# Normed tokens and gated values set off by several distances modulo 512 bytes from the weights they are multiplied with

## The chip, the cores and the metric

The kernel runs on one core of a Trainium2 chip. The metric is the device time of one execution in microseconds (us); the figure for a kernel is the median of several executions. The core has five engines that work side by side: TensorE (PE, with its weight loads shown apart as PEld), VectorE (DVE), ScalarE (ACT), GpSimd (POOL) and SyncE (SP), which here issues most of the DMA transfers. Data lies in SBUF, 128 partitions wide; TensorE takes both of its operands from there and writes to PSUM.

## The reference, cut to what matters

Two layers over 1024 latent and 256 context tokens, 1024 features wide, everything in fp32. What is multiplied is this:

```python
u = modulate(rms_norm(h, norm1_g), shift1, scale1)
p = u @ w_in                      # 1024 -> 2336 columns, cut into three mixers
y = ...                           # attention, long convolution, linear attention, a norm per head
h = h + gate1 * (y @ w_out)
u = modulate(rms_norm(h, norm2_g), shift2, scale2)
h = h + gate2 * ((silu(u @ ffn_w1) * (u @ ffn_w3)) @ ffn_w2)    # 1024 -> 2816 -> 1024
```

After the second layer a last norm gives the output for the latent tokens.

## The kernel before

**Products.** Features stand on partitions, in 8 chunks of 128. Every large product is made in three matmuls: each operand is split into a high and a low part in the format float32r (4 bytes an element), and `mm3` adds high by high, high by low and low by high. So a block of output, 128 features by up to 512 tokens, takes 8 chunks times 3, 24 matmuls, each with its own load of 128 by 128 weights (the stationary operand, 512 bytes a partition), while the tokens stream past (the moving operand, 2048 bytes a partition for 512 tokens). Tokens come in three blocks: 0 and 1 of 512 latent tokens, 2 of the 256 context tokens. The last layer has no context tokens in its second half.

**Tiles on the left side of SBUF.** Pools are opened and closed like a stack, and each begins where the one before it ends:

- `wts` (`open_w`): `hl`, two slots of 8 KB for streamed weights, high and low, and `raw`, 4 KB.
- `u0` (`open_u0`): the normed tokens of block 0, 32 KB.
- `u`: those of blocks 1 and 2, 32 KB and 16 KB.
- `w4`, in the second half of a layer alone (`phase34`): a third slot `hl` for `ffn_w1` and `ffn_w3`, two of `w2` for `ffn_w2`, and raw tiles.
- `g`, after it: the gated values silu(u w1) (u w3), high and low, two tiles.
- `w1`, in the first half of a layer (`phase1`): `tm`, weights of 288 columns that are the moving operand, with 128 tokens of `u` as the stationary one.

All these tiles are multiples of 512 bytes long, and so are their chunks, but for those of `tm`: 288 columns of 4 bytes are 1152 bytes, twice 512 and 128 more. So `hl`, `w2`, `u` and `g` begin at one and the same place modulo 512 bytes, and `tm` moves on by 128 from chunk to chunk.

**Stages.** For each layer `phase1` makes the input projection, `phase2` the three mixers, `phase34` the output projection (tiles `y`), the second norm and SwiGLU. In SwiGLU two hidden chunks are made (`hidden`: 24 matmuls of `u` by `hl` for each of w1 and w3 and each block), and their share of the output is added to the residual `h` (8 groups of 6 matmuls of `g` by `w2` a block). Every third weight tile of w1 and w3 goes to the slot in `w4`:

```python
for i, src in enumerate((A["ffn_w1"], A["ffn_w3"])):
    j = 2 * m + i
    ws.append(self.load_w(src[l][:, c], wp=wp if j % 3 == 2 else None, raws=wp if i else None))
```

Weights come by a DMA on SP's queue to `raw`; ScalarE makes the high part (L421), GpSimd the low part (L187), TensorE multiplies (L175). The order of the instructions on each engine is set by a scheduler in the framework, which simulates a timeline when the program is built. In the first layer VectorE also makes modulation vectors under SwiGLU (`ada_dve`, L329), which it sums over partitions by fp32 matmuls against ones (tiles `acc`, `ones`).

Of the kernel before, what the change touches and what calls it, by code (L numbers as in the profile page):

```python
# [17 lines left out]
P = 128  # L18
# [12 lines left out]
# columns of the combined input projection  # L31
C_Q, C_K, C_V, C_HY, C_GQ, C_GK, C_GV, C_GR, C_GF = 0, 512, 640, 768, 1536, 1664, 1792, 2048, 2304

# rows of the packed per-layer vectors
# [3 lines left out]
# ---------------------------------------------------------------- constants that depend on shapes alone  # L38
# [13 lines left out]
def _pk(m):  # L52
    """[T, K] -> [2, 128, T/128 * K]: exact parts, rows on partitions."""
    t, k = m.shape
    return np.stack([x.reshape(t // P, P, k).transpose(1, 0, 2).reshape(P, -1) for x in _hilo(m)])


def _consts():
    f = np.float64
    c = {}  # L60
# [25 lines left out]
    # rotations from the half-sample offset to offset 0, frequencies on partitions  # L86
# [37 lines left out]
class Builder:  # L124
# [20 lines left out]

    def ps(self, role=None):
        """a bank of PSUM: of a role, or of the current roles in turn."""
        role = self.role if role is None else role
        if role is None:
            role = self.cyc[self.nps % len(self.cyc)]  # L150
            self.nps += 1
        banks = self.banks[role]
        self.turn[role] = (self.turn[role] + 1) % len(banks)
        return self.psum.tile([P, 512], F32, name=self.nm("ps"), tag=f"ps{banks[self.turn[role]]}", bufs=1)

    def roles(self, *banks):
        """the banks of PSUM that each role takes in turn."""
        self.banks, self.turn = banks, [-1] * len(banks)

    def act_table(self, name):  # L160
        """one activation table set from here on: ScalarE's later instructions stay behind its load."""
# [11 lines left out]
    # -------------------------------------------------------------- small helpers  # L173
# [3 lines left out]
    def mm3(self, out, w, x, start, stop):  # L177
        """w, x: pairs (hi, lo); out += whi xhi + whi xlo + wlo xhi."""
# [10 lines left out]
    def rsqrt(self, pool, v, n, tag, eps=None, bufs=2):  # L189
        """-2 / sqrt(v + eps) for v [128, n] in PSUM: exp(-ln/2) and a Newton step."""  # L190
# [13 lines left out]
    # -------------------------------------------------------------- setup  # L204
# [42 lines left out]
    def vectors(self, vp, silb, ahead):  # L247
        """the conditioning vectors, biases and gains, features on partitions; other loads go ahead in between."""
        nc, A = self.nc, self.A
        for srcs in ((("c", None, 8), ("c_ctx", None, 8)),  # L250
# [22 lines left out]
            elif "filt_b1" in at:  # L273
                nc.vector.tensor_copy(self.fvec, ps[:, 0:3])
                # the norm gains scaled by -1/2: rsqrt() returns -2 / sqrt
# [6 lines left out]
    # -------------------------------------------------------------- adaLN vectors  # L282
# [10 lines left out]
    def ada_pe(self, l, part, wp, silb, ahead=()):  # L293
        """mod vectors: the conditioning vectors (16 columns each) stationary, weights moving; the rows of weights in
        turn on three column tiles."""
# [20 lines left out]
    def ada_dve(self, l, part, half, wp):  # L316
        """mod vectors of half a part: weighted rows summed on the vector engine; returns what sums the partitions."""
# [27 lines left out]
    # -------------------------------------------------------------- modulated norm: u (hi, lo) per block of tokens  # L345
    def norm_scale(self, l, which):
        """[128, 8, 2] gains: -1/2 g (1 + scale)."""
# [8 lines left out]
    def square(self, h, k, n, tp, acc):  # L356
        """adds the squares of chunk k of h [128, 8, n]; returns the sum so far, and whole, 1 / rms: tokens on partitions."""
# [23 lines left out]
    def spread(self, r, n, tp):  # L381
        """r [128, n / 128] -> -2 r of each token on all partitions, in PSUM."""
# [7 lines left out]
    def norm_u(self, h, u, scale, shift, r, tp, pool=(), tags=("s", "acc")):  # L390
        """u [128, 2, 8, n] F32R from h [128, 8, n]; r: -2 / rms; pool: the chunks whose low parts GpSimd makes."""
# [14 lines left out]
    # -------------------------------------------------------------- weights  # L406
    def load_w(self, src, n=P, wp=None, raws=None, lo_eng=None):
        """src [1024, n] -> (hi, lo) tile [128, 2, 8, n]."""
# [15 lines left out]
    # -------------------------------------------------------------- tokens in: feature-major residual  # L424
    def load_h(self, hp, xp):
        """features on partitions; yields after each block, with its -2 / rms on all partitions (PSUM)."""
# [35 lines left out]
    # -------------------------------------------------------------- hyena filters  # L462
    def sin_arg(self, pool, ps, b, fr, n):
        """sin(fr * (ps + b)) [128, n], the argument brought to [-pi, pi]."""
# [13 lines left out]
    def filter_mlp(self, fp, up):  # L478
        """hidden features of both layers' filters (a layer on 64 partitions), latent and context lengths, to DRAM."""
# [28 lines left out]
    def filter_body(self, l, kinds, fp):  # L508
        """spectra of one layer's filters to DRAM, latent ('l') and context ('c') lengths."""
# [5 lines left out]
        # X = [h_hi; h_lo], W1 = [w_hi; w_hi], W2 = w_lo  # L515
# [9 lines left out]
        def times(job):  # L525
            """the filter of a job in time, taken apart into folded levels."""
# [36 lines left out]
        def spectra(job, levels):  # L563
# [3 lines left out]
            for group in self.groups(levels):  # L567
                for pair, ps in self.transform(group, dft, fp):
                    for i, (L, k) in enumerate(pair):
# [20 lines left out]
                        else:  # L590
                            # cosine twice, or the two of the cyclic level; then the sine of either
# [26 lines left out]
    def start(self, hp, sp, up, tp, u):  # L618
        """tokens in, the first modulation vectors, the hidden features of the filters, the first norm."""
# [38 lines left out]
    # -------------------------------------------------------------- input projection  # L658
    def phase1(self, l):
        """norm 1, the input projection and what follows it token by token."""  # L660
# [3 lines left out]
        with ExitStack() as es:  # L664
            u = []
            if l == 0:
                self.open_w()
                self.open_u0()
            if l == 0:
                up = es.enter_context(self.pool("u", reuse_waits="tile"))  # L670
                hp = self.hpool.__enter__()
# [20 lines left out]
            # feature-major columns  # L692
# [11 lines left out]
            # hyena: short convolution  # L704
# [21 lines left out]
            # gated linear attention: gates (silu as x sigmoid(x)), queries, keys  # L726
# [47 lines left out]
    def open_w(self):  # L774
        """room of the streamed weights."""
# [8 lines left out]
    def open_u0(self):  # L784
        """room of the first block of the normed tokens."""
        self.u0p = self.pool("u0", 1, reuse_waits="tile")
        self.up0 = self.u0p.__enter__()

    def norm1(self, l, b, r, up):
        """norm 1 of a block of layer l > 0."""  # L790
# [4 lines left out]
    def load_tm(self, srcs, wp=None):  # L795
        """column groups side by side: [128, 2, 8, n]."""
# [15 lines left out]
    def tm(self, u, hl, n, tci):  # L812
        """tokens of chunk tci on partitions: [128, n] in PSUM."""
# [9 lines left out]
    def log_sigmoid(self, e, out, ps, m=None, b=None):  # L823
        """out = min(x, 0) - ln(1 + exp(-|x|)), x = ps + b; e, m: room."""
# [10 lines left out]
    def gla_prep(self, l, last, gv, tp, u):  # L835
# [27 lines left out]
        # decays: cumulative log gates of each chunk of 128 tokens, centred on its middle  # L863
# [4 lines left out]
        for d in range(2):  # L868
# [15 lines left out]
            # from the centre of a chunk to that of the next one  # L884
# [16 lines left out]
    def qkv(self, l, last, W, tp, u):  # L901
# [14 lines left out]
        def heads(ps, nh, which, tci, out, scale):  # L916
            """RMS norm, gain and rotation of nh heads: out [128, nh, 64]."""
# [7 lines left out]
            # scale / sqrt(ss / 64 + eps)  # L925
# [16 lines left out]
        def feature_major(xs, dst, c0):  # L942
            """token-major [128, 128] tiles of consecutive chunks from c0 on to dst [128, tokens] in DRAM."""
# [32 lines left out]
    # -------------------------------------------------------------- heads' norm and the mixed output  # L976
    def headnorm(self, tp, o, chunk, b0, n, l, v=None, gate=None, q=None):
        """o [128, n] (two heads of 64): RMS norm per head, gain, optional gate; to y_d. v: the mean squares if known."""
# [15 lines left out]
    # -------------------------------------------------------------- attention  # L994
    def attn_kv(self, ap, kvh):
        """operands of one kv head: K1 = [k_hi; k_lo], K2 = [k_hi; 1]."""
# [14 lines left out]
    def attn_q(self, ap, h, ops, b):  # L1011
        """operands of a block of queries: Q1 = [q_hi; q_hi], Q2 = [q_lo; -max]."""
# [27 lines left out]
    def attn_o(self, ap, ops, b, Q):  # L1040
        """softmax and values of a block of queries, two heads at once: the unnormalized outputs, one bank, and the
        sums of the weights over each partition's keys."""
# [28 lines left out]
    def attention(self, l, last, ap, np_):  # L1071
# [15 lines left out]
        for i, (kvh, pr, b) in enumerate(jobs):  # L1087
# [4 lines left out]
            # eps times the squares of the sums, on the partitions of each head  # L1092
# [13 lines left out]
    # -------------------------------------------------------------- hyena  # L1106
# [26 lines left out]
    def halves(self, s, L, tile):  # L1133
        """difference and sum of the halves of s [128, 2 L]: the negacyclic and the cyclic part."""
# [6 lines left out]
    def fold(self, f, d, L, cyc):  # L1141
        """d [128, L] about its middle: what the cosines see, then what the sines see."""
# [14 lines left out]
    def groups(self, levels):  # L1157
        """levels (L, folded): L of a negacyclic level, 0 for the cyclic one of 256; the two smallest go together."""
        return [[x] for x in levels[:-2]] + [levels[-2:]]

    def transform(self, group, dft, hp):
        """half-sample-offset transforms of a group: pairs of 128 frequencies, (cosine | sine) [128, 256] each, in PSUM."""
# [28 lines left out]
    def hyena_conv(self, l, kind, n, t0, order, hf, z, dft, hp):  # L1191
        """z <- x * (conv(z) + bias z) for one half of the channels, [128, n]."""
# [20 lines left out]
        for group in self.groups(levels):  # L1213
# [29 lines left out]
            # back to channels on partitions: the cosine and the sine part of each level  # L1243
# [46 lines left out]
    # -------------------------------------------------------------- gated linear attention  # L1290
    def gla(self, l, last, gp, np_):
# [11 lines left out]
        # states before each chunk, scaled to its centre: a head on 32 partitions  # L1303
# [32 lines left out]
        for c0 in range(0, 8 if last else 10, 2):  # L1336
            # masked scores of two chunks, both directions: a bank per head
# [34 lines left out]
    def phase2(self, l):  # L1372
        """the mixers: the hyena and the linear attention in turn, the attention wherever the engines are free."""
# [23 lines left out]
    # -------------------------------------------------------------- output projection  # L1397
    def phase34(self, l):
        """the output projection, norm 2 and SwiGLU; for the next layer's norm 1, its first block; or the output."""
# [3 lines left out]
        self.open_u0()  # L1403
# [215 lines left out]
```

## Time and profile before

| | |
|---|---|
| device time, median of 3 executions | 3714.42 us (3711.81 to 3720.55) |
| span of the profiled execution | 3712.2 us |
| mean granted TensorE clock | 0.978 of full speed |
| busy: PE, PEld, DVE, ACT, POOL | 3563.2, 2693.5, 2014.1, 1088.0, 1353.5 us |

The span runs from the first to the last instruction of the execution that the profiler took; the median lies 2.2 us above it, within the spread of the three executions. A matmul's recorded length reaches from its start to its modelled end, and matmuls overlap, so the step from one to the next is read from runs: the time of a run of n matmuls, less the length of the last, through n - 1. Full speed is 2.4 GHz, the other level of the clock (0.5 in the rows) 1.2 GHz; at full speed 512 columns take 213.3 ns at one column a cycle.

### The profile page before, as it was taken

To read this page: it belongs to the slowest core of one execution; us is meant where nothing else is said; L and a number is where in the kernel's file an instruction comes from. 1 tells how busy PE (TensorE), PEld (TensorE's weight loads), DVE (VectorE), ACT (ScalarE), POOL (GpSimd) and SP (SyncE) were. 2 spreads that over 40 slices of the span, in tenths; PEclk is the share of its full clock that TensorE was granted. 3 is DMA by queue.
4 is the path that set the end of the run, shared out by engine and by line. 5 is a ranking of instruction groups with operands and counts; after the bars stand their busy time and mean duration, and the time that the engine had idled before them with its cause. 6 is when DMAs were issued, how large, how long until landed. Compare 5 with 4: busy or idle time off the path is not lost.

```text
span 3712.2 us, 46254 instructions
## 1 busy us (share of the span) xinstructions
PE 3563.2 (96%) x17903; PEld 2693.5 (73%) x17903; DVE 2014.1 (54%) x3271; ACT 1088.0 (29%) x1956; POOL 1353.5 (36%) x960
## 2 busy tenths in 40 slices
PE   8999899999999999999999899899999999999999
PEld 4789845445677888888888688865445788888887
DVE  6755667863677665644223773757753533223233
ACT  4243233553422111111111333333554421111112
POOL 2424564664333111111111541656764542221221
PEclk9999999999999999999999899999999999999999
DMA  9333311120633323321111333411112421111111
GB/s 329 99 124 123 120 33 43 56 81 20 212 110 99 95 80 89 90 66 54 49 35 46 107 111 116 150 49 42 35 70 71 139 63 51 40 57 46 52 40 57
DMA packets 275804, 310.63 MB, mean 84 GB/s; under 512 B 18680, under 2 KB 205727, under 8 KB 274304
## 3 DMA queue, kind: packets, MB, share of 16 engines
q1 hardware_dynamic: 269279, 287.75, 24.6%
q0 software_dynamic: 2560, 13.89, 1.0%
q10 hardware_dynamic: 3744, 6.03, 0.4%
q8 instruction: 140, 2.29, 0.3%
q14 instruction: 81, 0.66, 0.1%
HBM read 245.75 MB, written 61.87 MB: 83 GB/s over the span
## 4 chain that ended last, share of the span: by engine, by line
PE 75%; DVE 11%; POOL 4%; issue 3%; DMA 3%; ACT 1%; SPq 0%; DVEq 0%; POOLq 0%; ACTq 0%
PE ps L175 74%; PE ps L184 1%; POOL hss L928 1%; DMA nsq<-in_ada_w 1%; POOL hl L187 1%; DVE acc L329 1%; DVE mx L1032 1%; DVE sg L1138 1%; DMA yr<-y_d 0%; DVE h L1537 0%; POOL hy L936 0%; DVE sg L1150 0%; DVE sg L1151 0%; DVE nacc L365 0%; DVE hx L930 0%
## 5 line engine op out<-in xcount | busy, mean ns | idle before, releaser
L175 PE MATMUL ps<-u,hl 128*128 128x512 f32 (+1 forms) x6504 | 1384.4, 372 | 20.6 <-DVE u L403 6.2
L175 PEld LDWEIGHTS ps<-u,hl 128*128 128x128 f32 x6504 | 1136.3, 190 | 252.5 <-issue 14.9
L187 POOL TENSOR_TENSOR hl<-raw,hl 128x1024 fp32r<-128x1024 f32 x148 | 366.5, 2479 | 944.3 <-ACT hl L421 924.5
L175 PE MATMUL ps<-g,w 128*128 128x512 f32 (+1 forms) x2688 | 556.6, 367 | 10.0 <-DVE h L1537 3.4
L175 PEld LDWEIGHTS ps<-g,w 128*128 128x128 f32 x2688 | 466.6, 190 | 95.5 <-DVE h L1537 5.4
L1068 POOL TENSOR_TENSOR ac<-ac,p 128x512 f32<-128x512 f32 x256 | 354.7, 1394 | 159.4 <-ACT p L1057 158.8
L1498 DVE TENSOR_TENSOR s<-ps,s 128x512 f32<-128x512 f32 (+1 forms) x110 | 70.0, 637 | 614.7 <-PE ps L175 597.3
L1537 DVE SCALAR_TENSOR_TENSOR h<-ps,mod,h 128x512 f32<-128x512 f32 (+1 forms) x448 | 303.5, 687 | 181.8 <-PE ps L175 181.6
L175 PE MATMUL ps<-p,V 128*64 128x512 f32 x672 | 309.8, 607 | 4.7 <-ACT p L1057 2.5
L187 POOL TENSOR_TENSOR w<-raw,w 128x1024 fp32r<-128x1024 f32 x44 | 109.0, 2477 | 500.0 <-ACT w L421 499.9
L1032 DVE TENSOR_REDUCE mx<-ps 128x1 f32<-128x512 f32 (+1 forms) x400 | 221.0, 587 | 120.8 <-PE ps L175 119.8
L1057 ACT ACTIVATE p<-ps 128x512 f32<-128x512 f32 (+1 forms) x336 | 194.6, 586 | 286.8 <-PE ps L175 277.7
L175 PEld LDWEIGHTS ps<-Q,K 65*128 65x128 f32 (+1 forms) x672 | 105.0, 191 | 222.2 <-issue 209.8
L421 ACT CAST hl<-raw 128x1024 fp32r<-128x1024 f32 x148 | 154.9, 1049 | 303.9 <-PE ps L175 151.5
L329 DVE SCALAR_TENSOR_TENSOR acc<-nsq,silc,acc 128x512 f32<-128x512 f32 x252 | 210.6, 876 | 61.3 <-DMA nsq<-in_ada_w 60.6
L175 PE MATMUL ps<-Q,K 65*128 65x512 f32 (+1 forms) x672 | 242.2, 442 | 1.2 <-ACT p L1057 1.1
L175 PE MATMUL ps<-y,hl 128*128 128x512 f32 (+1 forms) x960 | 213.8, 381 | 13.2 <-DVE y L187 6.1
L175 PEld LDWEIGHTS ps<-y,hl 128*128 128x128 f32 x960 | 170.8, 194 | 59.3 <-DVE y L187 8.2
L421 ACT CAST w<-raw 128x1024 fp32r<-128x1024 f32 x44 | 46.2, 1051 | 491.8 <-PE ps L175 443.2
L175 PE MATMUL ps<-my,dft 128*128 128x256 f32 (+1 forms) x1176 | 166.8, 294 | 10.3 <-DVE my L187 9.7
L1499 ACT CAST g<-s 128x512 fp32r<-128x512 f32 (+1 forms) x110 | 63.3, 576 | 385.2 <-DVE s L1498 385.2
L175 PEld LDWEIGHTS ps<-my,dft 128*128 128x128 f32 x1176 | 159.1, 203 | 20.6 <-DVE my L187 13.7
(265 smaller groups left out, 4129.2 us busy)
## 6 DMA issues: line engine op xcount, KB each, us to landing
raw<-in_ffn_w SPq DMA_DIRECT2D x132, 512.0 KB
nsq<-in_ada_w SPq DMA_DIRECT2D x144, 256.0 KB
raw<-in_w_in SPq DMA_DIRECT2D x36, 512.0 KB
raw<-in_w_out SPq DMA_DIRECT2D x32, 512.0 KB
ada<-in_ada_w SPq DMA_DIRECT2D x24, 512.0 KB
h_d<-h SPq DMA_DIRECT2D x32, 256.0 KB
dft<-in_c_dft POOLq DMA_DIRECT2D x8, 1024.0 KB, 7.2
qd<-qT_d SPq DMA_DIRECT2D x64, 128.0 KB
```

Source lines behind the costliest of these rows:

```text
L175: self.nc.tensor.matmul(out, w, x, start=start, stop=stop)
L184: self.nc.tensor.transpose(out, in_, self.ident[:n, :n])
L187: eng.tensor_tensor(out=out, in0=x, in1=hi.bitcast(F32), op=ALU.subtract)
L329: nc.vector.scalar_tensor_tensor(out=acc[w], in0=raw, scalar=s, in1=acc[w], op0=ALU.mult, op1=ALU.add)
L421: self.nc.scalar.copy(hi, raw)
L928: nc.gpsimd.tensor_tensor(out=ss, in0=ss, in1=self.mh[:, :nh], op=ALU.pow)
L1032: nc.vector.tensor_reduce(out=mx[:, j, i:i + 1], in_=pm, op=ALU.max, axis=AX.X)
L1057: nc.scalar.activation(p, st, AF.Exp)
L1068: nc.gpsimd.tensor_tensor(out=acc[j], in0=x, in1=ps[j], op=ALU.add)
L1498: nc.vector.tensor_tensor(out=s, in0=p3, in1=s, op=ALU.mult)
L1499: nc.scalar.copy(gs[m][:, 0, o:o + n], s)
L1537: nc.vector.scalar_tensor_tensor(out=h, in0=ps, scalar=self.mod[l][:, 40 + k, w:w + 1], in1=h, op0=ALU.mult, op1=ALU.add)
```

## The change

A helper puts a small tile, filled with zeros by GpSimd, at the bottom of a pool, so that all that lies above it moves up by that many bytes. It is called at eight places: for `u0` and `u` of the first layer's `phase1`, and for `u0`, `u` and `g` in each layer's `phase34`. (The diff also strips comments and docstrings, left out here.)

```diff
+AT = (32, 128, 256, 384, 64, 192, 448, 320)
...
+    def shift(self, pool, n, tag="shift"):
+        if n:
+            self.nc.gpsimd.memset(self.t(pool, [P, n // 4], F32, tag, 1), 0.0)
...
# phase1
-                self.open_u0()
+                self.open_u0(AT[0])
             if l == 0:
                 up = es.enter_context(self.pool("u", reuse_waits="tile"))
+                self.shift(up, (AT[1] - AT[0]) % 512)
...
-    def open_u0(self):
+    def open_u0(self, at):
         self.u0p = self.pool("u0", 1, reuse_waits="tile")
         self.up0 = self.u0p.__enter__()
+        self.shift(self.up0, at)
...
# phase34
-        self.open_u0()
+        self.open_u0(AT[2 + 3 * l])
...
             up = self.upc.__enter__()
+            self.shift(up, (AT[3 + 3 * l] - AT[2 + 3 * l]) % 512)
...
             gp = es.enter_context(self.pool("g", 2, reuse_waits="tile"))
+            self.shift(gp, AT[4 + 3 * l])
```

The distances that follow, in bytes modulo 512, of the tokens or values from the weights:

| stage | `u0` | `u1`, `u2` | `g` from `w2` |
|---|---|---|---|
| layer 0, `phase1` | 32 | 128 | |
| layer 0, `phase34`, and layer 1, `phase1` | 256 | 384 | 64 (`phase34`) |
| layer 1, `phase34` | 192 | 448 | 320 |

They hold against `hl` in `wts`. The pools above `u` move with it, so the third slot `hl` in `w4` has `u1` and `u2` at distance 0, as before, and `u0` at 384 (layer 0) and 256 (layer 1).

## Rows read from the trace of the kernel before

**Rows 1.** The page: busy time by engine, and the chain that ended last

```profile
PE 3563.2 (96%) x17903; PEld 2693.5 (73%) x17903; DVE 2014.1 (54%) x3271; ACT 1088.0 (29%) x1956; POOL 1353.5 (36%) x960
...
PE 75%; DVE 11%; POOL 4%; issue 3%; DMA 3%; ACT 1%; SPq 0%; DVEq 0%; POOLq 0%; ACTq 0%
```

**Rows 2.** Groups of instructions on PE by form, whole span

```profile
line engine op names shapes xcount | busy us, mean ns | idle before us <-releasers
L175 PE MATMUL ps<-u,hl 128*128 128x512 f32 x5184 | 1223.6, 394 | 17.7 <-DVE u L403 5.7 <-ACT u L402 4.1 <-DVE acc L397 3.5
L175 PE MATMUL ps<-g,w 128*128 128x512 f32 x2064 | 474.7, 390 | 2.5 <-DVE h L1537 2.2 <-DVE mod L341 0.3
...
L175 PE MATMUL ps<-u,hl 128*128 128x256 f32 x1320 | 170.6, 284 | 2.9 <-ACT u L402 1.6 <-DVE u L403 0.5 <-POOL u L187 0.4
...
L175 PE MATMUL ps<-hl,u 128*128 128x256 f32 x912 | 118.3, 289 | 0.0
...
L175 PE MATMUL ps<-g,w 128*128 128x256 f32 x624 | 83.9, 292 | 7.5 <-ACT s L1497 2.3 <-DVE g L187 1.6 <-DVE h L1537 1.2
L175 PE MATMUL ps<-tm,u 128*128 128x288 f32 x480 | 65.9, 299 | 4.2 <-ACT tm L421 3.7 <-POOL tm L187 0.4
```

**Rows 3.** Busy time in stretches of the two SwiGLU stages, with the granted clock

```profile
core 0: us, PE busy (x) PEld busy (x) DVE busy (x) ACT busy (x) POOL busy (x), PEclk, DMA share, GB/s
...
1100.00:2080.00 980.00, 960.55 (x4920) 806.79 (x4919) 511.59 (x722) 173.80 (x268) 200.47 (x101) 0.99 0.24 71
...
2965.00:3712.20 747.20, 737.23 (x3368) 613.78 (x3366) 243.03 (x323) 139.66 (x194) 171.99 (x77) 1.00 0.17 51
```

**Rows 4.** Timeline of PE, four runs at full clock: start, busy us, count

```profile
3299.86 5.83 PE L175 MATMUL ps<-u,hl 128*128 128x512 f32 x25
...
287.74 3.50 PE L175 MATMUL ps<-tm,u 128*128 128x288 f32 x25
...
331.81 3.28 PE L175 MATMUL ps<-hl,u 128*128 128x256 f32 x26
...
1299.82 2.56 PE L175 MATMUL ps<-g,w 128*128 128x256 f32 x20
```

**Rows 5.** Line L175: least, median and greatest length (ns) of loads and matmuls

```profile
L175 PEld LDWEIGHTS ps<-u,hl x6504: 186/188/338, 70.1 to 3663.2; 128*128 128x128 f32 x198
L175 PE MATMUL ps<-u,hl x6504: 274/389/793, 70.1 to 3663.4; 128*128 128x512 f32 x159, 128*128 128x256 f32 x39
```

**Rows 6.** Timeline of PE, a run at the lower clock

```profile
1126.26 5.49 PE L175 MATMUL ps<-u,hl 128*128 128x512 f32 x12 [1.48 <-DVE u L403]
```

**Rows 7.** Busy time and granted clock of that run

```profile
1126.86:1131.40 4.54, 4.54 (x12) 3.57 (x11) 4.54 (x7) 1.20 (x2) 3.50 (x3) 0.50 0.05 10
```

**Rows 8.** Timeline of PE behind fp32 matmuls: the first ten, then eleven

```profile
1302.43 1.08 PE L175 MATMUL ps<-acc,ones 128*64 128x512 f32 x4
...
1303.77 2.47 PE L175 MATMUL ps<-u,hl 128*128 128x512 f32 x10
...
1305.85 2.65 PE L175 MATMUL ps<-u,hl 128*128 128x512 f32 x11
```

**Rows 9.** Groups of POOL memsets, whole span

```profile
L768 POOL MEMSET zt<- 128x260 f32 x8 | 2.2, 317 | 1.9 <-DMA gk_d<-t 1.9
L218 POOL MEMSET ones<- 128x128 f32 x1 | 0.2, 205 | 0.3 <-POOLq L1607 0.3
...
L222 POOL MEMSET epsb<- 128x1 f32 x1 | 0.1, 99 | 0.0
```

**Rows 10.** Groups on POOL from 1060 to 1180 us

```profile
L187 POOL TENSOR_TENSOR hl<-raw,hl 128x1024 fp32r<-128x1024 f32 x10 | 24.8, 2482 | 35.9 <-ACT hl L421 30.1 <-PE ps L175 5.7
L187 POOL TENSOR_TENSOR u<-acc,u 128x512 fp32r<-128x512 f32 (+1 forms) x12 | 15.2, 1278 | 0.0
```

## The prediction

> **What bounds the kernel now.** I read the page first: TensorE is busy for 3563.2 of 3712.2 us and holds 75% of the chain that ended last, almost all of it line L175 [rows 1]. Next the groups by form: which products hold that time. Tokens by weights (`u` by `hl`) and gated values by weights (`g` by `w`) in blocks of 512 are 5184 and 2064 matmuls with 1223.6 and 474.7 us, those in blocks of 256 another 1320 and 624; with the 912 of `hl,u` they are 10,104 matmuls, and the idle time in front of any of these groups is at most 17.7 us [rows 2]. By stage, TensorE is busy for 960.55 of 980 us and 737.23 of 747.2 us in the two SwiGLU stages, nearly all of it at full clock [rows 3]. So nothing but the pace of a matmul counts there, and 1 ns on each of those matmuls is 10 us.
>
> Then the pace itself, from runs on the timeline [rows 4]. 25 matmuls of 512 columns take 5.83 us; less the last one's 0.389 us [rows 5] that is 5.441 us through 24, 226.7 ns a step. 512 columns at 2.4 GHz would be 213.3 ns, so 13.4 ns are over. 288 columns of `tm`: (3.50 - 0.30) / 24 = 133.3 ns against 120, 13.3 over. 256 columns of `hl,u`: (3.28 - 0.289) / 25 = 119.6 against 106.7, 12.9 over; of `g,w`: (2.56 - 0.292) / 19 = 119.4, 12.7 over. (The last lengths are the groups' means [rows 2].) The surplus is the same for 256, 288 and 512 columns: it goes with the matmul or its weight load, not with the columns. At the lower clock it is gone: 12 matmuls in 5.49 us, the last of them 0.79 us long [rows 5, 6], make 427 ns a step, at a granted clock of 0.50 [rows 7], and 512 / 1.2 GHz is 426.7 ns. So the surplus is no fixed number of TensorE cycles. It looks like two reads of SBUF that get in each other's way at full speed. That is what a displacement could relieve, if the addresses modulo 512 decide it.
>
> **The change part by part.** *Addresses.* Nothing is computed otherwise: the same matmuls, loads and transfers, with `u` and `g` moved. Three rows speak on what that is worth. First, `tm`: its chunks are 1152 bytes apart, so against `u` its distance already goes through 0, 128, 256 and 384 from chunk to chunk; were the collision one of equal places modulo 512, three matmuls in four would go without it, and the mean step of the run would be about 120 + 13.3 / 4 = 123.3 ns. It is 133.3 [rows 4], the same surplus as where every distance is 0. Second, a load is on record for 188 ns of each 226.7 ns step [rows 5]; in that time the moving operand advances by some 1700 bytes and the weights by 512 (an estimate from these two rows). The two reads drift past each other by more than twice 512 bytes during one load, so a start 32 or 448 bytes further on only changes when they meet, not how often. Third, the pace does depend on something in time: behind fp32 matmuls the first steps are irregular, (2.47 - 0.39) / 9 = 231.1 ns over ten, and the next eleven are back at (2.65 - 0.39) / 10 = 226.0 [rows 8]. The stream falls into one rhythm by itself, within about ten matmuls, from whatever phase it starts. I take 0 ns a matmul. The bounds are 13.3 ns saved (all of the surplus) and 231.1 - 226.7 = 4.4 ns lost (no rhythm at all).
>
> [...]
>
> *Which matmuls move.* By the loops, 1008 of the 6504 of `u` by `hl` keep distance 0 (blocks 1 and 2 against the third slot: 336 for each of two blocks in layer 0, 336 in layer 1). The other 5496, the 2688 of `g` and the 912 of `hl,u` are 9096. Of these and of `tm`, those whose distance is no multiple of 128, which `tm` says nothing about, are: `g`, 2688; `u0` in layer 0's first half, 240 + 192 + 192; in layer 1's SwiGLU `u0` and `u1` against the two slots in `wts`, 2 times 720. Together 4752.
>
> *Eight memsets on GpSimd.* They are 8 to 80 columns wide, between 99 ns for one column and 205 ns for 128 [rows 9]: 0.8 to 1.6 us in all. A gain is excluded. GpSimd has room where the second norm and SwiGLU begin: 35.9 us idle in front of its ten `hl` splits in 120 us [rows 10]. If a memset waited there for the tile that held its bytes before, the splits behind it (2.48 us each) would be late, and TensorE for them; but the first bytes of `u0`, `u` and `g` belong to tiles that were read to the end before these pools open, so I take 0, with 2.5 us (one split) for each of the six in `phase34`, 15 us, as the other bound.
>
> *Order.* The scheduler builds the queues from a simulated timeline, and eight new instructions can change places elsewhere. No row prices that; TensorE idles for 3712.2 - 3563.2 = 149 us in all [rows 1], outside the matmul streams, and I allow a twentieth of that either way, 7 us.
>
> The sum: 3712.2 + 0 + 0 + 0 = 3712 us by the profiled execution, 2.2 us below the median of the runs; so 3714 us beside the median.
>
> **Rivals.**
>
> *No collision by equal places.* If the surplus is lost only at distance 0, the 9096 save 13.3 ns each: 121 us, 3593. For it: the surplus vanishes at half the clock [rows 6, 7]. Against it: `tm` [rows 4]. Should only the fine distance (below 128) matter, 4752 save 13.3 ns, 63 us, 3651; `tm` does not speak against this, only the drift during a load does. A part of that (a shorter rhythm, some ns) would land between 3651 and 3706.
>
> *The rhythm is lost.* The steady 226.7 ns are what the stream settles into with equal places. If another distance doesn't let it settle, it goes on at the 231.1 ns of the steps behind fp32 matmuls [rows 8]: 4.4 ns on 4752 matmuls is 21 us, 3735; on all 9096, 40 us, 3754. It decides as soon as the mean step rises by 0.8 ns over 9096 (7.4 us). For it: the irregular steps exist. Against: 25 `tm` matmuls with four distances keep the rhythm [rows 4].
>
> *A memset in the way.* GpSimd held in `phase34` for up to 15 us: 3729.
>
> *The change does little of what it says.* For blocks 1 and 2 and every third weight tile the distance stays 0; that alone would take only 1008 out of 10,104 from any effect, so it decides nothing.
>
> **How the numbers follow.** No effect of the addresses, with the order's 7 us either way: 0.52, own range 3707 to 3722. Faster: all of the surplus 0.05 (3593), the fine distances 0.10 (3651), part of it or a luckier order 0.11 (3655 to 3706). Slower: rhythm lost on some or all 0.13 (3722 to 3754), memset or order 0.09 (3722 to 3735). A measurement of this kernel can tell about 0.2%, 7.4 us, from no change: so faster 0.26, same 0.52, slower 0.22. The range reaches from 3650 to 3740; it leaves out the full surplus and the upper end of the lost rhythm, about 1 in 10.
>
> **What would show it.** The run of 25 `u,hl` matmuls in layer 1's SwiGLU (distances 192 and 448) should again take 226.7 ns a step, that of `g,w` the same at 64 and 320; `u1` against the third slot is the control at distance 0 inside the same stage. Eight new memsets of 0.1 to 0.2 us should stand on GpSimd, with no idle time at their semaphores. I am wrong if the step at some distance is below 224 or above 229 ns, or if the idle time of TensorE between the stages moves by more than 7 us.

## The result, and the profile after

The changed kernel took 3742.0 us (median of 4 executions, 3735.51 to 3743.99), the kernel before on the same chip 3713.11 us (4, 3711.76 to 3720.55). The two medians differ by 28.9 us. The ratio is 1.0066, with a 95% interval of 1.0051 to 1.008: slower by 0.5 to 0.8%. (Here and below the ratio is the one on record with its interval, not the quotient of the two medians; the two differ by up to 0.13%.) The forecast was 3714 us, and the range ended at 3740.

The page of the changed kernel, with the lines that answer to [rows 1]:

```profile
span 3742.2 us, 46262 instructions
...
PE 3593.5 (96%) x17903; PEld 2692.5 (72%) x17903; DVE 2016.3 (54%) x3271; ACT 1088.2 (29%) x1956; POOL 1352.9 (36%) x968
...
PE 77%; DVE 11%; POOL 3%; issue 2%; DMA 2%; ACT 1%; SPq 0%; DVEq 0%; POOLq 0%; ACTq 0%
```

The span is 30.0 us longer and TensorE is busy for 30.3 us longer, with the same 17903 matmuls; its idle time is what it was (148.7 us, 149.0 before). The time went into the matmuls themselves. Which ones, the groups by form tell, beside [rows 2]:

```profile
L184 PE MATMUL ps<-u,hl 128*128 128x512 f32 x5184 | 1244.2, 398 | 18.2 <-DVE u L412 6.1 <-ACT u L411 4.5 <-DVE acc L406 3.4
L184 PE MATMUL ps<-g,w 128*128 128x512 f32 x2064 | 482.1, 394 | 2.4 <-DVE h L1550 2.1 <-DVE mod L350 0.3
...
L184 PE MATMUL ps<-u,hl 128*128 128x256 f32 x1320 | 170.2, 284 | 2.9 <-ACT u L411 1.6 <-DVE u L412 0.5 <-POOL u L196 0.4
...
L184 PE MATMUL ps<-hl,u 128*128 128x256 f32 x912 | 116.8, 287 | 0.0
...
L184 PE MATMUL ps<-g,w 128*128 128x256 f32 x624 | 82.6, 289 | 7.9 <-ACT s L1510 2.4 <-DVE g L196 1.5 <-DVE h L1550 1.2
L184 PE MATMUL ps<-tm,u 128*128 128x288 f32 x480 | 65.8, 299 | 3.7 <-ACT tm L430 3.1 <-POOL tm L196 0.6
```

Blocks of 512 tokens cost 20.6 us more as `u` by `hl` and 7.4 us more as `g` by `w`; the forms with 256 columns cost less, 0.4, 1.5 and 1.3 us; `tm` is as before. That is 24.8 of the 30.3 us. The rest can't be told from scatter: the products of attention that were not moved, `p` by `V`, are busy for 304.9 us before, 306.9 us here, and 309.0 us in the first experiment below, where no distance changes.

The timeline of PE shows the steps behind these sums, one run to a line (start, busy us, count), in the order of the list below:

```profile
3073.74 10.43 PE L184 MATMUL ps<-u,hl 128*128 128x512 f32 x44
...
3084.71 10.66 PE L184 MATMUL ps<-u,hl 128*128 128x512 f32 x45
...
1787.64 10.66 PE L184 MATMUL ps<-u,hl 128*128 128x512 f32 x45
...
1776.74 10.61 PE L184 MATMUL ps<-u,hl 128*128 128x512 f32 x46
...
1244.81 5.19 PE L184 MATMUL ps<-u,hl 128*128 128x512 f32 x22
...
3069.43 3.79 PE L184 MATMUL ps<-u,hl 128*128 128x512 f32 x16
...
1285.88 21.46 PE L184 MATMUL ps<-g,w 128*128 128x512 f32 x93
...
1373.70 21.63 PE L184 MATMUL ps<-g,w 128*128 128x512 f32 x92
...
2913.72 29.56 PE L184 MATMUL ps<-y,hl 128*128 128x512 f32 x126
```

Read as in the prediction (the run less its last matmul, of the group's mean length, through one matmul less; 0.404 us for `y`), the steps are: 233.3 ns at distance 192, 233.2 at 448, 233.2 at 384, 226.9 at 256, and 228.2 for a run of 22 of `u1` against the third slot, which kept distance 0. This is the control: it begins with some irregular steps (its first eight matmuls take 2.01 us, 230.3 ns a step) and then settles (its last eleven, from 1247.57 us on, take 2.66 us, 226.2 ns), as in the 16 matmuls of the next line, of a later run of the same kind (3.79 us, less 0.389, through 15: 226.7 ns). `g` at distance 64 steps by 229.0 ns in one pair of chunks and by 233.4 ns in the next: one distance, two rhythms. The last line is `y` by `hl` in layer 1, 233.2 ns; more on it below.

The eight memsets are one group on POOL, 0.9 us in all, with 0.2 us of idle time in front of them:

```profile
L153 POOL MEMSET shift<- 128x64 f32 (+6 forms) x8 | 0.9, 131 | 0.2 <-PE ps L184 0.2
```

### The profile page after: what moved, and what is told of

Same layout as the page of the kernel before. It is cut to its first block, busy times and chain, and to the rows that moved or that the text cites. A ratio compares the mean times of both kernels' runs of the same rounds, so it can differ in the third digit from the quotient of the medians.

```text
span 3742.2 us, 46262 instructions
## 1 busy us (share of the span) xinstructions
PE 3593.5 (96%) x17903; PEld 2692.5 (72%) x17903; DVE 2016.3 (54%) x3271; ACT 1088.2 (29%) x1956; POOL 1352.9 (36%) x968
## 4 chain that ended last, share of the span: by engine, by line
PE 77%; DVE 11%; POOL 3%; issue 2%; DMA 2%; ACT 1%; SPq 0%; DVEq 0%; POOLq 0%; ACTq 0%
PE ps L184 76%; PE ps L193 1%; POOL hss L939 1%; DMA nsq<-in_ada_w 1%; DVE acc L338 1%; DVE mx L1043 1%; POOL hl L196 1%; DVE sg L1149 1%; DVE h L1550 0%; POOL hy L947 0%; DVE sg L1161 0%; DVE sg L1162 0%; DVE hx L941 0%; DMA yr<-y_d 0%; DVE hx L950 0%
## 5 line engine op out<-in xcount | busy, mean ns | idle before, releaser
L184 PE MATMUL ps<-u,hl 128*128 128x512 f32 (+1 forms) x6504 | 1404.5, 375 | 21.1 <-DVE u L412 6.6
L430 ACT CAST hl<-raw 128x1024 fp32r<-128x1024 f32 x148 | 154.9, 1048 | 302.1 <-PE ps L184 152.9
```

Of the source, the lines that this page charges most:

```text
L184: self.nc.tensor.matmul(out, w, x, start=start, stop=stop)
L430: self.nc.scalar.copy(hi, raw)
```

## The experiments

The theory formed on this profile: *the distance modulo 512 between the moving operand and the weights that are loaded beside it sets the rhythm of a series of matmuls; for 512 columns 0 and 256 keep the step of 226.7 ns, other distances cost 2 to 7 ns.* (All these weights lie at multiples of 512 bytes from each other, so the runs can't tell those that are being loaded from those in use.) Rivals: the memsets and the new order of instructions; the place of an operand by itself; any displacement at all. Eleven kernels ran. Each edit is against the changed kernel, and ratios are to the kernel before in the same series of runs.

**Memsets and order without distances.** Seven zeroed tiles, 512 bytes each.

```diff
         if n:
+            n = 512
             self.nc.gpsimd.memset(self.t(pool, [P, n // 4], F32, tag, 1), 0.0)
...
# layer 0, phase1
-                self.shift(up, (AT[1] - AT[0]) % 512)
```

> Seven of the eight zeroed tiles stay (the one of u in layer 0's first half has no room), but each is 512 bytes long, so every distance is 0 as in the kernel before, while the memsets and a new order of instructions are there. If the distances make the loss: 3713 us, within 7. If the memsets or the order make it: 3735 or more, with steps of 226.7 ns for 512 columns and idle time of TensorE 20 us or more above the 149 us of before.

Measured 3717.12 us against 3715.94, ratio 1.001 (0.9999 to 1.0022). The groups of the wide blocks are back at the 1223.6 and 474.7 us of [rows 2]:

```profile
L185 PE MATMUL ps<-u,hl 128*128 128x512 f32 x5184 | 1223.1, 394 | 17.7 <-DVE u L413 5.7 <-ACT u L412 4.2 <-DVE acc L407 3.5
L185 PE MATMUL ps<-g,w 128*128 128x512 f32 x2064 | 474.7, 390 | 2.5 <-DVE h L1550 2.2 <-DVE mod L351 0.3
```

The rival of memsets and order is out.

**Weights moved along.**

```diff
-AT = (32, 128, 256, 384, 64, 192, 448, 320)
+AT = (0,) * 8
...
         self.wp = self.wpc.__enter__()
+        self.shift(self.wp, 192)
```

> No tile is set off from its weights; instead the pool of the weights, at the bottom, and with it all that lies above (hl, raw, u0, u, y, w2, g, tm) moves up by 192 bytes. If the distance between the two operands sets the step: 226.7 ns for 512 columns and 3713 us, within 7. If the start of an operand by itself (its place modulo 512) sets it: 231 to 233 ns as at 192 in the changed kernel, and 3740 or more.

Measured 3716.5 us, ratio 1.0003 (0.9991 to 1.0014). In layer 1's SwiGLU (groups on PE from 2960 us on) the busy time is that of before, 228.1 ns a matmul of `u` by `hl`; the first line is the kernel before, the others this run:

```profile
L175 PE MATMUL ps<-u,hl 128*128 128x512 f32 x2112 | 481.9, 389 | 0.2 <-POOL u L187 0.2
...
L184 PE MATMUL ps<-u,hl 128*128 128x512 f32 x2112 | 481.8, 389 | 0.2 <-POOL u L196 0.2
L184 PE MATMUL ps<-g,w 128*128 128x512 f32 x1008 | 230.4, 389 | 0.0
```

So it is how the operands lie to each other that counts.

**One distance for all.** Four kernels, with one number in the table.

```diff
-AT = (32, 128, 256, 384, 64, 192, 448, 320)
+AT = (256,) * 8
```

> u0, u, y and g all at distance 256 from their weights (the third slot in w4 at 0). If the distance counts modulo 256: 226.7 ns a step for 512 columns, 120 ns for 256 columns, 3713 us, up to 3 more. If any displacement costs what the changed kernel lost: 231 ns or more and 3740 us or more.

> u0, u, y and g all at distance 64 (u against the third slot in w4 at 0). Distance theory, from the steps of the changed kernel at 64, 192 and 448: 3840 matmuls of u by hl with 512 columns at 6.2 ns more, 2064 of g by w at 4.7 to 6.5, 768 of y by hl at 5.8, less some 3.5 us for 256 columns: 36 us, 3749 us (3742 to 3755). If order or memsets made the loss: no relation to the distance, within 10 us of 3742 or 3713.

> u0, u, y and g all at distance 192 (u against the third slot in w4 at 0). In the changed kernel 512 columns took 233.3 ns a step at 192 and at 448, in the run at 64 a repeating 226, 229, 232 (229). If 192 has its own, slower rhythm: 3840 matmuls of u by hl, 2064 of g by w and 768 of y by hl at some 6.5 ns more, 43 us above the kernel before, less what 256 columns give back (up to 10 us): 33 to 43 us above. If the changed kernel's steps came from the mixture of distances and not from 192: within 10 us of the kernel before, as at 64.

> u0, u, y and g all at distance 128 (u against the third slot in w4 at 0). From the changed kernel's 232.8 ns at 128 and 384: 6672 matmuls of 512 columns at 5.7 ns more, 38 us, less some 2 us for 256 columns: 30 to 38 us above the kernel before. If that came from the mixture: within 10 us.

| distance | median, before | ratio (95%) |
|---|---|---|
| 256 | 3720.23, 3715.94 | 1.0005 (0.9994 to 1.0017) |
| 64 | 3720.88, 3715.94 | 1.0013 (0.9999 to 1.0028) |
| 192 | 3751.05, 3717.68 | 1.0094 (1.0079 to 1.0109) |
| 128 | 3744.88, 3717.68 | 1.0086 (1.0065 to 1.0107) |

256 and 192 came out as the theory had it, and 128 nearly so: a displacement as such costs nothing that can be told from noise, and 192 and 128 cost 33.4 and 27.2 us between the medians, where 33 to 43 and 30 to 38 were expected. That is about what the mixture of the changed kernel cost, whose interval overlaps with both. At 64 the expectation of 3749 was wrong. The timeline of PE in that run says why; the lines are `u` by `hl`, `g` by `w` twice, and `g` by `w` with 256 columns twice:

```profile
3057.88 21.45 PE L184 MATMUL ps<-u,hl 128*128 128x512 f32 x93
...
1367.81 21.40 PE L184 MATMUL ps<-g,w 128*128 128x512 f32 x91
...
1455.24 21.45 PE L184 MATMUL ps<-g,w 128*128 128x512 f32 x93
...
1390.21 5.46 PE L184 MATMUL ps<-g,w 128*128 128x256 f32 x45
...
1477.21 5.38 PE L184 MATMUL ps<-g,w 128*128 128x256 f32 x46
```

With last lengths of 0.39 and 0.28 us: 228.9, 233.4, 228.9 ns a step for 512 columns; 117.7 and 113.3 ns for 256. I had carried 233.3 ns from 192 and 448 to 64, where `u` had never been; at 64 a quicker rhythm of 228.9 ns exists, and `u` falls into it. And 256 columns can go at 113.3 ns, 6.7 ns below the 120 of distance 0. By the groups of [rows 2], the wide blocks of `u` and `g` cost 12.2 us more than before and the narrow ones 6.3 us less; 4.9 us are left between the medians, in an interval that just includes no change.

Two rhythms at one distance are not peculiar to 64. In the run at 128, `g` with 512 columns steps by 232.4 ns in one pair of chunks and by 233.4 ns in another:

```profile
1363.94 21.31 PE L184 MATMUL ps<-g,w 128*128 128x512 f32 x91
...
1540.22 21.16 PE L184 MATMUL ps<-g,w 128*128 128x512 f32 x90
```

**A distance that changes.** The prediction had taken from `tm` that a distance going through 0, 128, 256 and 384 costs nothing. Here `u` does that with 512 columns, in layer 1's SwiGLU alone.

```diff
+AT = (0,) * 8
...
-            u[b] = self.t(up, [P, 2, KC, n], F32R, f"u{b}")
+            u[b] = self.t(up, [P, 2, KC, n + (32 if last else 0)], F32R, f"u{b}")[:, :, :, :n]
```

> Distances as before, but in layer 1's SwiGLU the chunks of u lie 2176 bytes apart in place of 2048, so the distance from the weights runs through 0, 128, 256 and 384 from chunk to chunk, as it does in tm. If a changing distance evens out, as the prediction took from tm: 226.7 ns a step of u by hl there. If each distance keeps its own step also for the three matmuls of one chunk: about the mean of 226.7 and 232.8, 229.8 ns, 6 us more in 2112 matmuls.

A single execution took 3723.51 us; the reading rests on the groups and not on that time. The groups on PE from 2960 us on:

```profile
L184 PE MATMUL ps<-u,hl 128*128 128x512 f32 x2112 | 493.0, 394 | 0.1
L184 PE MATMUL ps<-g,w 128*128 128x512 f32 x1008 | 231.0, 389 | 0.0
```

493.0 / 2112 is 233.4 ns a matmul, 5.3 ns more than the 228.1 with the distance held; the sum is 11 us, not the 6 expected of a mean over the four. What `tm` shows for its 288 columns does not hold for 512.

**A sweep.** `g` alone, at another distance in each pair of hidden chunks.

```diff
+AT = (0,) * 8
+GD = ((0, 16, 32, 48, 80, 96, 112, 144, 160, 176, 208), (128, 224, 240, 272, 288, 304, 352, 384, 416, 448, 480))
...
-                    gs[m] = self.t(gp, [P, 2, nt], F32R, "g")
+                    at = GD[l][m // 2] // 4
+                    gs[m] = self.t(gp, [P, 2 * nt + 128], F32R, "g")[:, at:at + 2 * nt].rearrange("p (s n) -> p s n", s=2)
```

> u and y at distance 0 as before; g lies at another distance from w2 in each pair of hidden chunks, 0, 16, 32, 48, 80, 96, 112, 144, 160, 176, 208 in layer 0 and 128, 224, 240, 272, 288, 304, 352, 384, 416, 448, 480 in layer 1. If the distance sets the rhythm: 226.7 ns for 512 columns at 0 alone, 229 to 234 ns elsewhere, 113 to 120 ns for 256 columns, and like steps at distances 256 apart. If only lines of 64 bytes count, 16, 32 and 48 would step alike.

A single execution took 3723.4 us. Runs on the timeline of PE at distances 0, 16, 32, 112, 160, 272, 288 and 416, then 256 columns at 16, 80 and 112:

```profile
1186.20 6.08 PE L185 MATMUL ps<-g,w 128*128 128x512 f32 x26
...
1278.95 21.94 PE L185 MATMUL ps<-g,w 128*128 128x512 f32 x94
...
1366.19 22.10 PE L185 MATMUL ps<-g,w 128*128 128x512 f32 x94
...
1710.41 21.89 PE L185 MATMUL ps<-g,w 128*128 128x512 f32 x94
...
1879.45 22.17 PE L185 MATMUL ps<-g,w 128*128 128x512 f32 x94
...
3211.29 21.94 PE L185 MATMUL ps<-g,w 128*128 128x512 f32 x94
...
3277.08 22.10 PE L185 MATMUL ps<-g,w 128*128 128x512 f32 x94
...
3540.88 22.41 PE L185 MATMUL ps<-g,w 128*128 128x512 f32 x95
...
1301.32 5.41 PE L185 MATMUL ps<-g,w 128*128 128x256 f32 x45
...
1563.59 5.20 PE L185 MATMUL ps<-g,w 128*128 128x256 f32 x42
...
1732.72 5.26 PE L185 MATMUL ps<-g,w 128*128 128x256 f32 x45
```

In order, for 512 columns: 227.6 (with its irregular first steps), 231.7, 233.4, 231.2, 234.2, 231.7, 233.4, 234.3 ns. 16 and 272, 32 and 288, 160 and 416 agree to 0.1 ns: in these three pairs, as in 0 and 256 (226.7 and 226.9 ns), the pattern repeats every 256 bytes. 16 and 32 differ, so it is finer than 64 bytes. For 256 columns it is 116.6 ns at 16 and 113.2 ns at 112; not every distance is a gain for them, at 80 they stay at 120.0 ns. Each distance had one series here, so the numbers are steps that a distance can have; as 64 and 128 show, it can have another.

**`g` alone as in the changed kernel.**

```diff
+AT = (0, 0, 0, 0, 64, 0, 0, 320)
```

> u0, u and y back at distance 0, g as in the changed kernel (64 in layer 0, 320 in layer 1). If each product's step follows its own distance: u by hl at 227 ns; g by w at 229 or 233 ns for 512 columns, 5 to 9 us, less 1 to 3 us for 256 columns: 2 to 8 us above the kernel before, so that u and y carry most of the changed kernel's loss. If g carries it: 20 us or more.

Measured 3725.05 us against 3717.8, ratio 1.0016 (1.0002 to 1.0029), 6 us by the ratio. The group of `g` cost 8.3 us more than in [rows 2], that of `u`, which was not moved, 2.5 us more:

```profile
L184 PE MATMUL ps<-u,hl 128*128 128x512 f32 x5184 | 1226.1, 395 | 17.4 <-DVE u L412 6.1 <-ACT u L411 3.9 <-DVE acc L406 3.5
L184 PE MATMUL ps<-g,w 128*128 128x512 f32 x2064 | 483.0, 395 | 2.4 <-DVE h L1550 2.1 <-DVE mod L350 0.3
```

So `g` alone makes a fifth to a quarter of the loss, and most of the rest is `u`, whose group grew by 20.6 us in the changed kernel.

**Only the narrow blocks displaced.** `u2` and block 2 of layer 0's `g` 112 bytes off, all that is 512 columns wide at distance 0.

```diff
+AT = (0,) * 8
...
+    def u2(self, up, n):
+        return self.t(up, [P, 2 * KC * n + 128], F32R, "u2")[:, 28:28 + 2 * KC * n].rearrange("p (s k n) -> p s k n", s=2, k=KC)
...
+                    gt = self.t(gp, [P, 2048 if last else 2688], F32R, "g")
+                    g01 = gt[:, :2048].rearrange("p (s n) -> p s n", s=2)
+                    gs[m] = (g01, g01, None if last else gt[:, 2076:2588].rearrange("p (s n) -> p s n", s=2))
```

> All blocks of 512 tokens at distance 0; only the block of 256 context tokens, in u and in layer 0's g, lies 112 bytes off. From the sweep: 512 columns stay at 226.7 ns, 256 columns go from 120 to 113.3 ns in 1320 matmuls of u by hl and 528 of g by w, up to 12 us; a run that falls into the rhythm of 118 ns instead gives a third of that. So 4 to 12 us below the kernel before. If the block's displacement also disturbs the 512 columns that follow: no gain, or a loss.

Measured 3707.72 us against 3717.8 (12 and 25 executions), ratio 0.9977 (0.9966 to 0.9988). Groups on PE by form:

```profile
L187 PE MATMUL ps<-u,hl 128*128 128x512 f32 x5184 | 1223.7, 394 | 19.1 <-DVE u L415 6.6 <-ACT u L414 4.7 <-DVE acc L409 3.4
...
L187 PE MATMUL ps<-u,hl 128*128 128x256 f32 x1320 | 164.7, 279 | 2.9 <-ACT u L414 1.6 <-DVE u L415 0.5 <-POOL u L199 0.4
...
L187 PE MATMUL ps<-g,w 128*128 128x256 f32 x624 | 81.4, 287 | 7.8 <-ACT s L1514 2.6 <-DVE g L199 1.6 <-DVE h L1556 1.2
```

The wide blocks of `u` stay at [rows 2]'s 1223.6 us, the narrow ones of `u` and `g` take 5.9 and 2.5 us less. That is 8.4 us, and 0.0023 of 3717.8 is 8.6 us.

**And the long convolution.** The same, with the tiles `my` set off 192 bytes from the transform matrices.

```diff
                   self.pool("hy", 1, reuse_waits="tile") as hp):
+                self.shift(hp, 192)
```

> The same, and in the long convolution the tiles my, 192 bytes off the transform matrices. Its 1032 matmuls of my by dft with 256 columns go from 120 to between 113.3 and 118 ns where they run in series, 2 to 5 us; its 192 of 512 columns lose 1 us. 1 to 4 us below the run before this one; no difference if waits in that stage hide it.

Measured 3702.57 us, ratio 0.9968 (0.9955 to 0.998). The group of `my` by `dft` is busy for 146.1 us against 149.3 in the run before this one, but it scatters between 147.9 and 152.9 us in the kernels that leave `my` where it was. The two intervals overlap as well. So that this step adds to the other rests on the steps themselves; a series in the run before this one, then two in this one:

```profile
445.81 5.56 PE L187 MATMUL ps<-my,dft 128*128 128x256 f32 x45
...
443.42 5.27 PE L187 MATMUL ps<-my,dft 128*128 128x256 f32 x45
...
2546.96 4.64 PE L187 MATMUL ps<-my,dft 128*128 128x256 f32 x38
```

With last lengths of 0.28 us these are 120.0, 113.4 and 117.8 ns a step: the two rhythms that 256 columns had at 64. The loss of 1 us expected at 512 columns did not come: `dft` by `my` took 48.0 us against 47.9. Both versions are faster than the kernel before, by 0.2 to 0.3%.

## Why the prediction was wrong

**What bounds the kernel** was right: nothing but the pace of the matmuls moved, and it moved the time in full (TensorE busy for 30.3 us longer, its idle time 148.7 us against 149.0, the span 30.0 us longer).

**The failed step** is the worth of the addresses, "I take 0 ns a matmul". In its place the runs showed 6.5 to 6.6 ns a matmul more in series of 512 columns at distance 192, 384 and 448 (233.2 and 233.3 ns against 226.7), and 2.2 to 7.6 ns more at the other distances read, but for 256 (228.9 to 234.3 ns, and 226.9); the groups of `u` and `g` with 512 columns grew by 28.0 us. The prediction's own sign of being wrong, a step above 229 ns, came at 192, 384 and 448, while `u1` against the third slot, its control, settled at its old one. The 0 stood on three arguments.

- *`tm` keeps its surplus at distances 0, 128, 256 and 384, so the distance is nothing.* The row was read rightly, the step to the other products was not: the same sequence of distances with 512 columns took 233.4 ns a matmul in place of 228.1 (the changing distance).
- *The two reads drift past each other, so a start further on "only changes when they meet, not how often".* An argument from two durations alone. The sweep and the four uniform distances show steps that depend on the start (226.9 ns at 256, 234.3 at 416), and in the three pairs of the sweep that were read they repeat every 256 bytes, to 0.1 ns. That the two reads meet at all is the author's guess and was not shown.
- *The stream "falls into one rhythm by itself, within about ten matmuls, from whatever phase it starts".* At distance 0 it does, behind ten irregular steps (231.1 ns, then 226.0 [rows 8]), and at 256 a run of 46 steps by 226.9 ns; that it does so from every phase was not shown. At 64 there are two rhythms, 228.9 and 233.4 ns, in one and the same run, and two at 128.

The reading in front of these, that the surplus "is the same for 256, 288 and 512 columns", holds in the runs of the kernel before [rows 4] and not at 112: there it is 17.9 ns for 512 columns and 6.5 ns for 256 (steps of 231.2 and 113.2 ns). It is counted over 213.3 and 106.7 ns, the prediction's figures for one column a cycle. What the rows show of them is (5.49 - 0.79) / 11 = 427.3 ns a step of 512 columns at a granted clock of 0.50 [rows 5, 6, 7]; half of that, 213.6 ns, is an estimate for the full clock, and a quarter, 106.8 ns, one for 256 columns.

**The rival that came true** is the lost rhythm, which had 0.13. Its mechanism holds with one correction: at distance 192 the stream isn't left irregular, it has a rhythm of its own, slower for 512 columns (four stretches of ten matmuls in the run of 44, from 3073.74, 3077.71, 3079.81 and 3081.68 us on, take 2.50 us each, 233.6 ns a step). Its price was too low for 512 columns: 4.4 ns from the irregular steps ([rows 8] leave out the first of them: that run begins at 1303.44, not at 1303.77), measured 6.6 at 192 and 6.5 at 384 and 448. It was too high for 256 columns, where several distances are a gain (113.2 to 117.8 ns at 16, 64, 112 and 192 against 120; none at 80), which this rival left out. That the 28.9 us lie within its bounds of 21 and 40 us is thus in part luck: two errors of opposite sign. With so little weight on it, the range was cut at 3740, under its upper end of 3754.

**The count of what moves** missed `y`. Its pool lies above `u0`, so the output projection's operand moved too, by 256 in layer 0 and 192 in layer 1, where its step is 233.2 ns. With 384 matmuls at 6.5 ns that is 2.5 us (an estimate, against the steady step of the other products); the group as a whole grew by only 0.7 us, from 189.0 to 189.7.

**The other rivals.** The full gain at unequal places is out: the distances read in the sweep took 227.6 to 234.3 ns for 512 columns, none below 226.7, and for 256 columns the most was half of the surplus, 6.7 of 13.3 ns. A memset in the way is out: 0.9 us of work and 0.2 us of waiting, against the 0.8 to 1.6 and 0 to 15 that were written down. Order: 1.2 us between the medians with the memsets alone, within the 7 us allowed.

**Open.** Why 0 and 256 keep the quickest step read for 512 columns (226.7 and 226.9 ns), why 256 columns have a quicker one elsewhere (113.2 ns at 112 against 120 at 0), and what picks one of two rhythms at the same distance (228.9 and 233.4 ns at 64). The runs show that it is a matter of how two operands lie to each other (233.3 ns at 192, but 228.1 ns a matmul, as before, where the weights and all above them moved by 192 alike) and, in the pairs that were read (0 and 256; 16 and 272, 32 and 288, 160 and 416 to 0.1 ns), that it repeats every 256 bytes; that two reads of SBUF get in each other's way is argued and not shown.

## What to carry to other kernels

In this kernel TensorE is the bound (busy for 96% of the span), and where the tiles lie to each other was part of the step of its runs: 226.7 ns at distance 0, 234.3 at 416, for 512 columns. Where another kernel is bound like this, check the distance modulo 256 bytes of each moving operand from its weights before and after any change of allocation, and remember that a pool moves all that lies above it, as it moved `y` here. Choose it by shape: here 0 or 256 for 512 columns (226.7 and 226.9 ns) and 112 for 256 columns (113.2 ns against 120), with 0.2 to 0.3% for it. A row that shows no effect for one shape proves nothing for another (`tm` keeps 133.3 ns over four distances, 512 columns go from 228.1 to 233.4); where one kernel can sweep the number, one run replaces the argument, as far as one series at each distance goes.

## What was not expected of the hardware

The matmuls of float32r here, with a fresh load of weights each, do not step by one fixed surplus, as the four runs of the kernel before made it look ([rows 4], 12.7 to 13.4 ns over the prediction's figure of one column a cycle). The steps read range from 226.7 ns (0; 226.9 at 256) over 228.9 (64, in the quicker of its two rhythms) and 231.2 (112) to 234.2 and 234.3 ns (160, 416) for 512 columns, and from 113.2 (112) to 120 ns (0) for 256. The surplus over 213.3 and 106.7 ns thus goes from 13.4 to 21.0 ns for the wide form and from 13.3 down to 6.5 ns for the narrow one, with the same instructions.
